# Early transposes kept in x, row factors in two steps, and a hand-ordered end: a change at both ends of a hybrid decoder trunk

## The chip, the cores and the metric

The kernel runs on one core of a Trainium2 chip. The core has five engines with instruction queues of their own: TensorE (PE, with its weight loads shown as PEld), VectorE (DVE), ScalarE (ACT), GpSimd (POOL) and SyncE (SP). SP issues nearly all loads here, ACT issues stores. TensorE writes to PSUM; the other engines read PSUM or the on-chip memory SBUF. The metric is the device time of one execution in microseconds (us); lower is better. A change of less than 0.5% (about 7 us) is not told apart from none here.

## The reference

One layer of a hybrid block on a sequence of 1024 rows of width 1024, then a final normalisation:

```python
mod = jax.nn.silu(c) @ ada_w + ada_b
shift, scale, gate = jnp.split(mod, 3, axis=-1)
h = rms_norm(x, norm_w) * (1 + scale[:, None, :]) + shift[:, None, :]
proj = h @ w_in
...  # two branches: y_a (gated spatial mixing) and y_b (state-space scan)
merged = jax.nn.sigmoid(g_a) * (y_a @ w_proj_a) + jax.nn.sigmoid(g_b) * (y_b @ w_proj_b)
return rms_norm(x + gate[:, None, :] * (merged @ w_out), final_norm_w)
```

The change touches the making of `h` and of the first products with `w_in` at the start, and the last product, `merged @ w_out`, with the final `rms_norm` at the end. The branches between are as before.

## The kernel before, in words

*Matrices and halves.* A row tile is 128 rows of x; there are eight (`xt[0]` to `xt[7]`), each with 1024 columns. The kernel needs h with its columns on the partitions, so every 128 x 128 piece is turned by a transpose on TensorE. A *block* is 128 columns of x; the eight blocks are worked in the order `KS = (0, 4, 1, 5, 2, 6, 3, 7)`, and "block n" below is place n of that order. A *half* `h` of a block is the row tiles 0 to 3 (`h = 0`) or 4 to 7 (`h = 1`). All products are made to fp32 precision from three products of a high and a low part, so that every row of h is also split in two (`hh`, `hl`).

*The first stage* (lines 168 to 457). `square(t)` sums the squares of a row tile on ACT, `factors` (L369) turns four sums at once into row factors with one small instruction on DVE (L371) and a power on POOL (L372), and `normed(t, half, eng)` (L374) scales 512 columns of a row tile in place (DVE L379 or ACT L377). `matvec(n)` multiplies 128 columns of the conditioning weights for shift and scale (`aw`, 1 MB a block in two buffers) on TensorE and copies the row; `modulation(n)` makes shift and scale of the block's columns from it. `transposes(n, h)` turns four pieces into a PSUM tile `px` (two buffers). `rows_of_h(n, h)` reads `px`, applies scale and shift in two ACT instructions (L297; for the very first block on DVE, L299 and L300), and subtracts to get the low part (DVE L301). `first_products(n)` is a generator of twelve products of a block, 128 x 512 each, six for a half; `split_w0(n)` prepares their weights (ACT L220, DVE L221).

The loop at L440 runs the twelve products of block n and, at set places between them, what block n + 1 needs (`prepare`, L403): for example `3: transposes(n, a)`, `5: modulation, rows_of_h(n, a)`, `9: transposes(n, b), rows_of_h(n, b)`, where a and b are the block's halves in the order in which it uses them. For block 1 a table of its own (L406) also holds the second half of block 0. The loads of block n + 2 are issued at the first product of block n. `warm(n)` issues products whose result nobody reads.

*What sets the order.* `pin` keeps an instruction in program order among the pinned ones of its engine. In the first stage nearly everything is pinned: its order on each engine is the order in the text. A planner lays out the instructions that are not pinned by a timing model; most of the vector, scalar and GpSimd work of the middle is of that kind. Waits between engines follow from the data, element by element; a tile's buffer goes to its next user when the last access has passed.

*The last stage* (L1651 to L1778). The last product is made as seven sub-products (`PRODUCTS`, L1711). Two of them matter here. `s4` completes columns 512 to 1023 of rows 0 to 511 (and the kernel finishes row tiles 4 to 7 beside it); `a12` completes columns 0 to 511 of row tiles 0 to 3 and is the last. `collect` (L1683) adds a PSUM tile to the row tile `r` on DVE and sums the squares on ACT; for row tiles 2 and 3 POOL multiplies the upper columns by the final weight `fnw` (L1691). `root(t)` makes one row factor with two 1-wide DVE instructions and a power on POOL (L1705 to L1707); `inv_root` (L1653) makes it on DVE by three Newton steps. `finish(t, y)` scales the row tile, whole on DVE (L1699) or, for tile 2, half on ACT (L1696) and half on DVE (L1697), and issues the store. Row tile 3 comes last, in two pieces of 256 columns (L1764 to L1778), with its factor by `inv_root`.

Of the kernel before, what the change touches and what calls it, by code (L numbers as in the profile page):

```python
# [16 lines left out]
P = 128  # L17
D = 1024
# [17 lines left out]
def hybrid_kernel(  # L36
# [131 lines left out]
    with tc.tile_pool(name="p0", bufs=1, reuse_waits="tile") as p0:  # L168
# [5 lines left out]
        xt = [p0.tile([P, D], F32, name=f"x{t}", tag=f"x{t}") for t in range(NCH)]  # L174
# [108 lines left out]

        def rows_of_h(n, h):
# [10 lines left out]
            if n + h:  # L295
                for t in (hh, hf):
                    pin(A.activation(t, px, AF.Identity, scale=md[:, 1:2], bias=md[:, 0:1]))  # L297
            else:
                pin(V.tensor_scalar(hf, px, md[:, 1:2], md[:, 0:1], op0=ALU.mult, op1=ALU.add))  # L299
                pin(V.tensor_copy(hh, hf))  # L300
# [68 lines left out]
        def factors(b):  # L369
            bs = slice(4 * b, 4 * b + 4)  # L370
# [69 lines left out]
        for n in range(KT):  # L440
            todo = prepare(n + 1) if n + 1 < KT else {}
            for at, _ in enumerate(first_products(n), 1):
                if at == 1 and n + 2 < KT:
# [1209 lines left out]
    def inv_root(n, w, other=None):  # L1653

        t, y, v = (dde[:, 8 * i + n : 8 * i + n + w] for i in range(3))
        if other is not None:
            V.tensor_scalar(t, part[:, n : n + 1], other, 1.0 / D, op0=ALU.add, op1=ALU.mult)
        else:
            V.tensor_add(t, part[:, n : n + w], part[:, 8 + n : 8 + n + w])
            V.tensor_scalar(t, t, 1.0 / D, EPS, op0=ALU.mult, op1=ALU.add)  # L1660
        V.tensor_scalar(y.bitcast(I32), t.bitcast(I32), -0.5, float(0x5F3759DF), op0=ALU.mult, op1=ALU.add)
        V.tensor_scalar_mul(v, t, -0.5)
        for _ in range(3):
            if w == 1:
# [148 lines left out]
```

## Time and profile before

| what | value |
|---|---|
| median of 3 runs | 1408.84 us (1404.32 to 1409.13) |
| the profiled execution | 1407.67 us, span 1405.9 us |
| TensorE busy | 1377.1 us, 98% of the span |
| DVE, ACT, POOL busy | 1062.4, 797.0, 213.0 us |
| granted TensorE clock, mean | 0.997 of full speed |
| data moved | 194.55 MB read, 87.46 MB written |

The span runs from the first to the last instruction of the trace; the profiled execution's own time is 1.8 us longer. A row of the trace in order of time gives the start in us, the duration, the engine, the line of the kernel, the operation, `output<-inputs`, the shape, and in brackets how long the engine had been idle and which work it had waited for. A line is often that of a helper (L81 is every product of the first stage, L84 every transpose, L90 every pinned load). `x4` means that four alike were merged. Instructions of one engine overlap a little at their ends, so that the distance between two starts is shorter than the duration. SPq and ACTq are the DMA issues of SP and ACT.

### The profile page before, as it was taken

How to read it: one execution, taken by the hardware profiler on the slowest of the kernel's cores; microseconds unless marked ns; L12 is line 12 of the kernel's file. 1: busy time of each engine (PE TensorE's matmuls, PEld its weight loads, DVE VectorE, ACT ScalarE, POOL GpSimd, SP SyncE). 2: the span in 40 equal slices, each digit the busy share in tenths (PEclk: the TensorE clock that was granted, in tenths of full speed). 3: DMA queues.
4: the chain of work that ended last, by engine and by line, in shares of the span. 5: the costliest groups of instructions: out<-in, count | busy, mean ns of one | idle time of the engine just before them, and what ended most of it. 6: DMA issues, size and time to landing. Idle time of an engine off the chain costs nothing.

```text
span 1405.9 us, 20633 instructions
## 1 busy us (share of the span) xinstructions
PE 1377.1 (98%) x7035; PEld 1139.9 (81%) x7035; DVE 1062.4 (76%) x1863; ACT 797.0 (57%) x1471; POOL 213.0 (15%) x208
## 2 busy tenths in 40 slices
PE   8999999999999999999999999999999999999997
PEld 6688888888888888888887888888888877878886
DVE  4786776777778889889788796388667767876976
ACT  5764576556656665556565555677766723322443
POOL 0000000000000011111000010038778740000001
PEclk9999999999999999999999999999999999999999
DMA  8653343343344777787675774598778749878903
GB/s 263 173 165 98 113 120 105 105 121 120 116 125 134 214 202 239 236 248 232 192 221 156 240 214 135 173 353 318 262 253 296 275 168 328 320 231 296 350 33 120
DMA packets 273150, 283.37 MB, mean 202 GB/s; under 512 B 15341, under 2 KB 223637, under 8 KB 273045
## 3 DMA queue, kind: packets, MB, share of 16 engines
q1 hardware_dynamic: 185684, 198.52, 44.4%
q10 hardware_dynamic: 87360, 83.54, 17.8%
q8 instruction: 55, 0.90, 0.3%
q14 instruction: 51, 0.41, 0.1%
HBM read 194.55 MB, written 87.46 MB: 201 GB/s over the span
## 4 chain that ended last, share of the span: by engine, by line
PE 80%; DMA 8%; DVE 5%; POOL 2%; issue 2%; ACT 1%; SPq 1%; ACTq 0%; DVEq 0%; POOLq 0%
PE xcb L574 6%; PE xuz L574 6%; PE xz L574 6%; PE xx L574 5%; PE xg L574 5%; PE x L1477 4%; PE yp L1477 4%; PE ox L1676 3%; PE yuz L574 3%; PE ycb L574 3%; PE pma L81 3%; PE xv L574 3%; PE yz L574 3%; PE yg L574 3%; PE yx L574 3%; DMA dcy<-acs_d 3%
## 5 line engine op out<-in xcount | busy, mean ns | idle before, releaser
L793 POOL TENSOR_TENSOR wog<-wog,gb 128x256 f32<-128x256 f32 x16 | 18.3, 1159 | 676.6 <-PE zz L574 413.3
L1007 ACT ACTIVATE dcy<-dcy,nacs 128x128 f32<-128x128 f32 x256 | 78.6, 388 | 14.9 <-POOL dcy L1002 14.5
L1002 POOL TENSOR_SCALAR_AFFINE_SELECT dcy<-dcy 128x1024 f32<-128x1024 f32 x32 | 35.0, 1095 | 135.7 <-ACT ea L999 132.3
L999 ACT ACTIVATE ea<-dcy 64x512 f32<-64x512 f32 x64 | 40.1, 626 | 14.2 <-DMA dcy<-acs_d 13.8
L920 ACT ACTIVATE ac<-ac 128x1024 f32<-128x1024 f32 x32 | 33.9, 1060 | 23.0 <-DVE ac L918 22.8
L81 PE MATMUL pma<-yh,wah 128*128 128x512 f32 x128 | 43.3, 419 | 0.0
L1027 DVE TENSOR_TENSOR dcy<-dcy,pc 128x1024 f32<-128x1024 f32 x32 | 39.0, 1218 | 4.8 <-PE pc L84 3.0
L81 PE MATMUL pma<-yh,wal 128*128 128x512 f32 x128 | 42.5, 413 | 0.0
L1089 POOL TENSOR_TENSOR yz<-y,sl 128x512 f32<-128x512 f32 x32 | 41.4, 1295 | 1.1
L1087 DVE TENSOR_TENSOR ym<-yn,ea 128x512 f32<-128x512 f32 (+1 forms) x32 | 19.9, 622 | 28.5 <-PE yn L81 28.3
L81 PE MATMUL pma<-yl,wah 128*128 128x512 f32 x128 | 40.1, 394 | 0.0
L1088 POOL TENSOR_TENSOR y<-y,ym 128x512 f32<-128x512 f32 (+1 forms) x32 | 36.6, 1144 | 14.4 <-DVE ym L1087 14.4
L81 PEld LDWEIGHTS yn<-sl,st 128*128 128x128 f32 x224 | 30.3, 190 | 8.3 <-issue 4.4
L81 PE MATMUL yn<-sl,st 128*128 128x128 f32 x224 | 31.6, 276 | 4.9 <-DVE st L1057 4.9
L1416 DVE SCALAR_TENSOR_TENSOR yn<-yn,par,rb 128x512 f32<-128x512 f32 x32 | 24.0, 749 | 15.7 <-DMA yn<-yb_d 15.5
L81 PE MATMUL sp<-xe,bn 128*128 128x256 f32 x112 | 32.6, 408 | 3.3 <-DVE ssq L1117 1.7
L81 PE MATMUL yi<-dcy,xd 128*64 128x128 f32 x512 | 35.7, 283 | 0.0
L918 DVE SCALAR_TENSOR_TENSOR ac<-c2x,cwt,ac 128x1023 f32<-128x1023 f32 (+2 forms) x24 | 31.2, 1300 | 5.3 <-ACT ac L916 5.1
L918 DVE SCALAR_TENSOR_TENSOR ac<-c2cb,cwt,ac 128x1023 f32<-128x1023 f32 (+2 forms) x24 | 31.1, 1296 | 4.4 <-ACT ac L916 4.3
L1691 POOL TENSOR_TENSOR r<-r,fnw 128x512 f32<-128x512 f32 x2 | 2.5, 1296 | 203.7 <-DMA out_dram<-r 203.7
L1055 POOL TENSOR_TENSOR st<-st,cd 128x256 f32<-128x256 f32 x48 | 32.1, 668 | 8.0 <-PE yn L81 5.3
L918 DVE SCALAR_TENSOR_TENSOR ac<-c1cb,cwt,ac 128x1023 f32<-128x1023 f32 (+2 forms) x24 | 31.6, 1318 | 1.3 <-ACT ac L916 1.3
(2980 smaller groups left out, 4390.9 us busy)
## 6 DMA issues: line engine op xcount, KB each, us to landing
sl<-s_d SPq DMA_DIRECT2D x32, 768.0 KB
s_d<-ac ACTq DMA_DIRECT2D x32, 512.0 KB
dcy<-acs_d SPq DMA_DIRECT2D x32, 512.0 KB
aw<-in_ada_w_dram SPq DMA_DIRECT2D x16, 512.0 KB
wbr<-in_w_proj_b_dram SPq DMA_DIRECT2D x64, 128.0 KB
wb_d<-wbb ACTq DMA_DIRECT2D x32, 256.0 KB
wb_d<-wbc ACTq DMA_DIRECT2D x32, 256.0 KB
yb_d<-yz ACTq DMA_DIRECT2D x32, 256.0 KB
```

What stands on the lines that cost most here:

```text
L81: pin(PE.matmul(acc, l, r, start=first, stop=last))
L574: pin(PE.matmul(ps, lw[:, k * P : (k + 1) * P], r[k], start=first and n + k == 0, stop=n == 2 and k == 3, skip_group_check=not first))
L918: V.scalar_tensor_tensor(ac[:, s:], cc[:, : S - s], conv_wt[:, 3 - s, i : i + 1], ac[:, s:], op0=ALU.mult, op1=ALU.add)
L920: A.activation(ac, ac, AF.Silu)
L999: A.activation(ea[hh * HD : (hh + 1) * HD], dcy.rearrange("p (j e) i l -> p e j (i l)", e=2)[hh * HD : (hh + 1) * HD, hh], AF.Exp)
L1002: G.affine_select(out=d8, in_=d8, compare_op=ALU.is_ge, fill=-1e30, base=0, pattern=[[0, 2 * HPG], [1, P]], channel_multiplier=-1)
L1007: A.activation(dcy[:, h, i, :], dcy[:, h, i, :], AF.Exp, bias=sub[:, i, h : h + 1])
L1027: V.tensor_tensor(d3, d3, pc[:, 0:256].unsqueeze(1).to_broadcast([P, HPG, 256]), op=ALU.mult)
L1088: G.tensor_add(y1[:, :, t0:], y1[:, :, t0:], m[:, :, t0:])
L1089: G.tensor_mul(yz, y1, sl[:, 4:6])
L1477: pin(PE.matmul(ps[j], a[:, v, js], r, start=first and n + k == 0, stop=n == 2 and k == KT - 1, skip_group_check=not first))
L1676: pin(PE.matmul(ps, a[:, tsl], b[:, cs], start=first and n + j == 0, stop=n == 2 and j == 3, skip_group_check=not first))
```

## The change

*Storage.* The eight tiles `xt` become two tiles of four row tiles each (`xq`); `xt[t]` is a view of them.

*Early transposes.* `turned(n, eng)` transposes half 0 of block n, and copies the PSUM tile back into x, over the columns it came from. It is called for blocks 2, 4, 1, 6, 3 and 5, ahead of the loop and between the first six products of block 0. The copies of 4 and 1 are on ACT, the others on DVE. In the loop, `transposes(n, 0)` is left out for blocks 1 to 6, and `rows_of_h(n, 0)` reads the copy in SBUF.

*Row factors.* `factors` takes a range: tiles 0 to 2 and then 3, tiles 4 to 6 and then 7. All scalings (`normed`) are now on DVE.

*Order of the first stage.* `matvec(0)` stands ahead of the scaling of the upper columns; the first six products of block 0 are drawn ahead of the loop; the second half of block 0 stands ahead of its seventh product; `matvec(1)` comes at the ninth product (it was the sixth), the rest of block 1 at the twelfth. There are 3, 5 and 4 warming products, where there were 3, 8, 6 and 5.

*The end.* POOL now multiplies the upper columns of row tiles 0 to 3 by `fnw`; `finish` splits tiles 0 to 3 between ACT and DVE; the last product `a12` is written out by hand and pinned, with each tile's finish one tile later than its sums; the last factor is a power on POOL in place of three Newton steps; for tile 3 only columns 0 to 255 are multiplied by `fnw` on POOL, 256 to 511 on DVE.

```diff
-        xt = [p0.tile([P, D], F32, name=f"x{t}", tag=f"x{t}") for t in range(NCH)]
+        xq = [p0.tile([P, 4, D], F32, name=f"xq{h}", tag=f"xq{h}") for h in range(2)]
+        xt = [xq[t // 4][:, t % 4] for t in range(NCH)]
...
+        four = lambda t: t.rearrange("p (i q) -> p i q", i=4)
+
+        def turned(n, eng):
+
+            transposes(n, 0)
+            part = xq[0][:, :, KS[n] * P : (KS[n] + 1) * P]
+            pin((A.copy if eng is A else V.tensor_copy)(part, four(pxs[n, 0])))
+            pxs[n, 0] = part
...
-                    pin(A.activation(t, px, AF.Identity, scale=md[:, 1:2], bias=md[:, 0:1]))
+                    pin(A.activation(four(t) if h == 0 and n in EARLY else t, px, AF.Identity, scale=md[:, 1:2],
+                                     bias=md[:, 0:1]))
...
-        def factors(b):
-            bs = slice(4 * b, 4 * b + 4)
+        def factors(a, b):
+            bs = slice(a, b)
...
-        for t in range(4):
-            square(t)
-        factors(0)
-        for t in range(4):
-            normed(t, 0, V)
+        for a, b in ((0, 3), (3, 4)):
+            for t in range(a, b):
+                square(t)
+            factors(a, b)
+            for t in range(a, b):
+                normed(t, 0, V)
         transposes(0, 0)
         split_w0(0)
+        matvec(0)
         for t in range(4):
             normed(t, 1, V)
-        matvec(0)
         warm(3)
         modulation(0)
-        warm(8)
+        turned(2, V)
+        warm(5)
         rows_of_h(0, 0)
+        start = first_products(0)
+        for i in range(6):
+            next(start)
+            if i == 1:
+                for t in range(4, 7):
+                    square(t)
+                factors(4, 7)
+                turned(4, A)
+            elif i == 3:
+                turned(1, A)
+            elif i == 5:
+                for n in (6, 3):
+                    turned(n, V)
+        for t in range(4, 7):
+            normed(t, 0, V)
+        turned(5, V)
+        square(7)
+        factors(7, 8)
+        for t in range(7, 8):
+            normed(t, 0, V)
         for t in range(4, NCH):
-            square(t)
-        factors(1)
-        for half in range(2):
-            for t in range(4, NCH):
-                normed(t, half, A if t > 5 else V)
-        split_w0(1)
+            normed(t, 1, V)
+        warm(4)
+        transposes(0, 1)
+        rows_of_h(0, 1)
+        EARLY = range(1, 7)
...
-                    6: lambda: (warm(6), transposes(0, 1), rows_of_h(0, 1), matvec(1), warm(5)),
-                    8: lambda: (transposes(1, 1), modulation(1), rows_of_h(1, 1)),
-                    12: lambda: (transposes(1, 0), rows_of_h(1, 0)),
+                    9: lambda: (matvec(1), split_w0(1), transposes(1, 1)),
+                    12: lambda: (modulation(1), rows_of_h(1, 1), rows_of_h(1, 0)),
...
+            early = lambda h: h == 0 and n in EARLY
...
-                3: lambda: transposes(n, a),
+                3: lambda: early(a) or transposes(n, a),
...
-                9: lambda: (transposes(n, b), rows_of_h(n, b)),
+                9: lambda: (early(b) or transposes(n, b), rows_of_h(n, b)),
...
-            if c and t in (2, 3):
+            if c and t < 4:
                 G.tensor_mul(r[:, cs], r[:, cs], fnw[:, cs])
...
-        if t == 2:
-            A.mul(r[:, 512:1024], r[:, 512:1024], y)
-            V.scalar_tensor_tensor(r[:, 0:512], r[:, 0:512], y, fnw[:, 0:512], op0=ALU.mult, op1=ALU.mult)
+        if t < 4:
+            pin(A.mul(r[:, 512:1024], r[:, 512:1024], y))
+            pin(V.scalar_tensor_tensor(r[:, 0:512], r[:, 0:512], y, fnw[:, 0:512], op0=ALU.mult, op1=ALU.mult))
...
+    def last_add(t, ps, cs, total):
+        r = rows[t]
+        pin(V.tensor_add(r[:, cs], r[:, cs], ps))
+        pin(A.activation(junk[:, cs], r[:, cs], AF.Square, accum_out=total))
+
+    lo, hi = slice(0, 256), slice(256, 512)
+    ps, r = acc["y"], rows[3]
+    for t in range(3):
+        for j in range(4):
+            out_products(ps[t], "a12", "b21", j, t, whole, True)
+        last_add(t, ps[t], whole, part[:, t : t + 1])
+        if t == 1:
+            finish(0, y0)
+        if t == 0:
+            y0 = root(0)
+        elif t == 1:
+            y1 = root(1)
+    for m, cs in enumerate((lo, hi)):
         for j in range(4):
             out_products(acc["xy"[m]][3][:, 0:256], "a12", "b21", j, 3, cs, True)
...
-    y = inv_root(3, 1, dde[:, 33:34])
-    V.tensor_scalar_mul(r[:, 0:512], r[:, 0:512], y)
+    finish(1, y1)
+    last_add(3, acc["x"][3][:, 0:256], lo, dde[:, 32:33])
+    y2 = root(2)
+    pin(G.tensor_mul(r[:, lo], r[:, lo], fnw[:, lo]))
+    pin(V.scalar_tensor_tensor(dde[:, 33:34], dde[:, 32:33], D * EPS, part[:, 11:12], op0=ALU.add, op1=ALU.add))
+    last_add(3, acc["y"][3][:, 0:256], hi, part[:, 3:4])
+    finish(2, y2)
+    v, y = dde[:, 34:35], dde[:, 35:36]
+    pin(V.tensor_scalar(v, part[:, 3:4], dde[:, 33:34], 1.0 / D, op0=ALU.add, op1=ALU.mult))
+    pin(G.tensor_tensor(y, v, nhalf[:, 0:1], op=ALU.pow))
+    pin(A.mul(r[:, 512:1024], r[:, 512:1024], y))
+    nc.scalar.dma_start(out[3 * P : 4 * P, 512:1024], r[:, 512:1024])
+    pin(V.scalar_tensor_tensor(r[:, hi], r[:, hi], y, fnw[:, hi], op0=ALU.mult, op1=ALU.mult))
+    pin(V.tensor_scalar_mul(r[:, lo], r[:, lo], y))
     nc.sync.dma_start(out[3 * P : 4 * P, 0:512], r[:, 0:512])
```

More of the change, by code (lines that the diff above doesn't have):

```diff
@@ L441, in hybrid_kernel @@
             todo = prepare(n + 1) if n + 1 < KT else {}
-            for at, _ in enumerate(first_products(n), 1):
-                if at == 1 and n + 2 < KT:
+            for at, _ in enumerate(first_products(n) if n else start, 1 if n else 7):
+                if at == (1 if n else 7) and n + 2 < KT:
                     load_aw(n + 2)
@@ L1651, in hybrid_kernel, with inv_root @@
     part = dthq[:, 0:16]
-    def inv_root(n, w, other=None):
+    def inv_root(n, w):
         t, y, v = (dde[:, 8 * i + n : 8 * i + n + w] for i in range(3))
[L1656 to L1660, printed above, removed]
+        V.tensor_add(t, part[:, n : n + w], part[:, 8 + n : 8 + n + w])
+        V.tensor_scalar(t, t, 1.0 / D, EPS, op0=ALU.mult, op1=ALU.add)
         V.tensor_scalar(y.bitcast(I32), t.bitcast(I32), -0.5, float(0x5F3759DF), op0=ALU.mult, op1=ALU.add)
@@ L1748, in hybrid_kernel @@
             continue
+        if nm == "a12":
+            break
         for t in range(4):
-            if nm == "a12" and t == 3:
-                break
             for j in range(4):
```

25 lines of the change are left out of this document (5 added, 20 removed).

## The prediction

> **What bounds the kernel now.** I read the page's head first, then the chain that ended last, then busy time by stretch, then the order of time at both ends of the kernel, which is where the diff is.
>
> ```profile
> span 1405.9 us, 20633 instructions
> PE 1377.1 (98%) x7035; PEld 1139.9 (81%) x7035; DVE 1062.4 (76%) x1863; ACT 797.0 (57%) x1471; POOL 213.0 (15%) x208
> PE 80%; DMA 8%; DVE 5%; POOL 2%; issue 2%; ACT 1%; SPq 1%; ACTq 0%; DVEq 0%; POOLq 0%
> 20.00:30.00 10.00, 9.05 (x67) 6.79 (x65) 3.90 (x11) 7.22 (x13) 1.02 (x1) 1.00 0.91 233
> 30.00:62.00 32.00, 31.82 (x243) 20.52 (x244) 23.76 (x52) 23.17 (x42) 0.00 (x0) 1.00 0.71 187
> ```
>
> The last two are rows of the view by stretches: length, then busy time of PE, PEld, DVE, ACT and POOL, the granted clock, DMA share and GB/s. TensorE carries the span (98%, 80% of the chain). From 30 to 62 us it is busy for 31.82 of 32 us, with DVE at 23.76 and ACT at 23.17: an instruction taken off PE there is time gained, as long as DVE and ACT follow. Before 30 us PE is filled up with warming products and waits for x, row factors and weights: there PE time is free, and the order on DVE, ACT and POOL counts. After PE's last product only a serial chain is left.
>
> **The change, head: how much it takes from PE.** Rows of PE in order of time, around one group of four transposes in block 1:
>
> ```profile
> 31.40 0.39 PE L81 MATMUL acc<-b22h,w0l 128*128 128x512 f32 x1
> 31.63 0.60 PE L84 MATMUL px<-ident,x 128*128 128x128 f32 x4
> 31.98 0.48 PE L81 MATMUL acc<-b22h,w0l 128*128 128x512 f32 x1
> ```
>
> Products come 0.23 apart (31.40 to 31.63); with the group between them, 0.58. A group thus costs 0.35 us. Six groups leave the block loop: that of block index 1 ran before 30 us, those of 2 to 6 ran in blocks 1 to 5, where PE is full. 5 x 0.35 = 1.75 us gained, if everything else keeps up. In exchange there are six copies (four on DVE, two on ACT) ahead of the loop, and rows_of_h then reads SBUF. Prices, from rows of the same shape a little later:
>
> ```profile
> 72.78 0.68 DVE L478 COPY dtt<-pd 128x512 f32<-128x512 f32 x1
> 75.41 0.58 ACT L590 COPY c1v<-xv 128x512 f32<-128x512 f32 x1
> 69.43 0.62 ACT L522 CAST p1v0h<-a11v 128x512 fp32r<-128x512 f32 x1
> ```
>
> A DVE copy out of PSUM is 0.68 (next one starts 0.60 later), an ACT one 0.58. An ACT read of SBUF is 0.62: 0.04 more, for twelve activations 0.5 us of ACT, hidden in its 9 idle us of the 32; if uncovered, one per block, 5 x 0.04 = 0.2 us. [...]
>
> **Head: what is late next.** The scalings, copies and factors are written out in order for each engine, so I follow DVE. Rows before:
>
> ```profile
> 10.04 0.19 ACT L367 ACTIVATION_READ_ACCUMULATOR junk<-x 128x1 f32 x1
> 11.89 1.03 POOL L372 TENSOR_TENSOR rs<-sq,nhalf 128x4 f32<-128x4 f32 x1 [10.16 <-DVE sq L371]
> 12.96 1.67 DVE L379 TENSOR_SCALAR x<-x,rs 128x512 f32<-128x512 f32 x4 [1.15 <-POOL rs L372]
> 16.71 0.41 DVE L263 COPY row<-pm 128x256 f32<-128x256 f32 x1
> 18.15 0.81 DVE L299 TENSOR_SCALAR hf<-px,md 128x512 f32<-128x512 f32 x1
> 18.99 0.43 DVE L300 CAST b11h<-hf 128x512 fp32r<-128x512 f32 x1
> 19.57 0.70 PE L81 MATMUL acc<-b11h,w0h 128*128 128x512 f32 x2
> 22.11 1.68 DVE L379 TENSOR_SCALAR x<-x,rs 128x512 f32<-128x512 f32 x4 [1.14 <-POOL rs L372]
> 24.87 0.77 ACT L297 ACTIVATE b<-px,md 128x512 fp32r<-128x512 f32 x1
> 28.84 0.49 PE L81 MATMUL acc<-b22h,w0h 128*128 128x512 f32 x1
> 30.07 1.07 PE L81 MATMUL pm<-aw,scz 128*32 128x256 f32 x16 [0.73 <-DMA aw<-in_ada_w_dram]
> 1390.60 0.55 POOL L1707 TENSOR_TENSOR dde<-dde,nhalf 128x1 f32<-128x1 f32 x1 [1.15 <-DVE dde L1706]
> ```
>
> *First tiles.* The third square ends at 10.23, the power on POOL takes 1.03 for four columns and 0.55 for one, so some 0.87 for three: three scalings of 0.42 run 11.43 to 12.68, the fourth, after its own factor (0.17 + 0.55 and hand-overs), ends at 13.90 instead of 14.63. That 0.7 us is spent again: DVE now holds its row copy until matvec(0) is through (15.3) with four scalings queued behind it (to 17.4), and the copy of block 2 (0.60) stands ahead of rows_of_h(0,0). Its cast then ends at 19.67 instead of 19.42: the first product runs at 19.8, 0.25 later.
>
> *Second tiles.* Before, DVE and ACT begin to scale x4..x7 at 22.11. After, PE has six products (0.23) with the groups of blocks 4, 1 and 6 (0.36) among them, from 19.8 to 22.3. DVE's queue holds, in this order, the copies of 6 and 3, three scalings, the copy of 5, the factor of tile 7 and only then the other scalings. So DVE, free at 20.6 and with the factors there at 21.6, waits for block 6's transposes until 22.45: copies to 23.65, scalings to 24.9, copy of 5 to 25.5, factor of tile 7 (0.17 + 0.55) to 26.4, its scaling to 26.8. transposes(0,1) end at 27.05 and ACT's first row of h starts there, not at 24.87: 2.2 us later. The 0.78 of that row gives the product at 27.9, matvec(1) behind three products at 28.6 (24 before); its row copy, w0's cast, modulation(1) and rows_of_h(1,1) bring block 1's first product to 32.4 against 28.84, and matvec(2) behind it to 32.6.
>
> What of it counts: before, matvec(2) stood at 30.07 for its weights anyway, so block 1 is late by 32.6 - 30.07 = 2.55, not 3.6. Against 1.75 gained, the head ends 0.8 us later. Bounds: no delay beyond the weights' arrival, -1.75; no gain left in the loop, +2.55. I take 0.8, which the rows add up to.
>
> *SP.* Loads for block index 3 wait for matvec(1) to release the buffer, so they are issued some 29.6 instead of 26. The load of index 2 took from 23.83, its issue, to 30.07, 6.2 us; 29.6 + 6.2 = 35.8, and matvec(3) wants it at 32.6 + 5.9 - 0.35 + 0.2 = 38.4. Queued behind it on SP are w0r of index 3, three small parameters and the loads of index 4: 2.6 us of cover; beyond that each microsecond costs one. Joining x into two tiles of four changes no address pattern that a load or product sees: nothing.
>
> **Tail.** Rows in order of time, before:
>
> ```profile
> 1395.84 1.28 DVE L1699 SCALAR_TENSOR_TENSOR r<-r,dde,fnw 128x1024 f32<-128x1024 f32 x1
> 1396.61 1.10 POOL L1771 TENSOR_TENSOR r<-r,fnw 128x256 f32<-128x256 f32 x1 [1.16 <-ACT junk L1770]
> 1396.62 0.28 PE L1676 MATMUL oy<-ms1h,mwhb 128*128 128x256 f32 x1
> 1397.04 0.68 DVE L1705 TENSOR_TENSOR dde<-dthq 128x1 f32<-128x1 f32 x1
> 1397.71 0.41 DVE L1769 TENSOR_TENSOR r<-r,oy 128x256 f32<-128x256 f32 x1
> 1398.21 0.42 ACT L1770 ACTIVATE junk<-r 128x256 f32<-128x256 f32 x1 [1.68 <-DVE dde L1706]
> 1398.89 1.19 DVE L1697 SCALAR_TENSOR_TENSOR r<-r,dde,fnw 128x512 f32<-128x512 f32 x1
> 1400.00 0.14 DVE L1661 TENSOR_SCALAR dde<-dde 128x1 int32<-128x1 int32 x1
> 1401.38 0.16 DVE L1669 SCALAR_TENSOR_TENSOR dde<-dde 128x1 f32<-128x1 f32 x1
> 1401.58 0.72 ACT L1777 ACTIVATE r<-r,dde 128x512 f32<-128x512 f32 x1 [2.02 <-DVE dde L1669]
> 1402.33 0.40 ACTq L1778 DMA_DIRECT2D out_dram<-r  x1
> ```
>
> PE's last product ends at 1396.90, but the last add starts at 1397.71, behind a 1024-wide finish and a 1-wide add that took 0.68 beside POOL's product. Then follow the square, a 1.19 us finish of row 2 and eight Newton steps (1400.00 to 1401.55). After: rows 0 to 2 are finished half on ACT (0.72) and half on DVE (some 0.64), so the last add can start at 1396.95 (+0.42), its square ends at 1397.9, row 2's half finish on DVE ends by 1398.0 (1398.5 if POOL slows it as in the 1.19 row), the sum 0.2, the power 0.55 with 0.1 of hand-overs: 1398.85 to 1399.35, ACT's product 0.72, and its store at 1399.6 to 1400.1 against 1402.33. That is -2.7 to -2.2; I take -2.5. Bounds: -2.8 with no contention; -1.5 where POOL's product of row 3 (up to 1.10) also holds the last add. The two further products on POOL and the ACT halves lie under PE's products of rows 0 to 2; uncovered they are 1.1 and 0.72 each.
>
> **Sum.** 1407.67 (the profiled execution: its span 1405.9 and 1.8 around it) + 0.8 - 2.5 = 1406.0. That execution lay 1.2 below the median 1408.84, so the median becomes 1407.1. The middle is untouched in the diff, yet what isn't pinned there is laid out by the planner anew: from the three runs shown (1404.32 to 1409.13) I allow 2 us either way.
>
> **The rivals.**
> *B, the head gains.* DVE's queue doesn't hold block 1 back; it starts where the weights of index 2 let it, as at 30.07. For it: the 0.73 wait on the DMA, and the freed ACT scalings. Against: the queue above. -1.75 - 2.5: 1404.6.
> *C, slower: the granted clock falls in the head.* At the end of the kernel it halves about 3 us after PE's last product:
>
> ```profile
> 1399.50:1400.00 0.50, 0.00 (x0) 0.00 (x0) 0.50 (x2) 0.06 (x1) 0.03 (x1) 0.89 0.00 0
> 1400.00:1402.00 2.00, 0.00 (x0) 0.00 (x0) 1.68 (x10) 0.42 (x1) 0.00 (x0) 0.50 0.54 217
> ```
>
> Between 23.7 and 27.9 PE would have only single transposes and four warming products, with 1.9 us empty at most; the clock before is 1.00 throughout 20 to 30. It decides once PE stands for 3 us. Products at half clock take 0.46: some 6 us of it until PE has been busy again cost 3 us: 1407.1 + 3 = 1410.1. [...]
> *D, the tail keeps its length.* POOL's product of row 3 and row 2's half finish meet, as in the 1.10 and 1.19 rows, and the planner's early finishes stay in DVE's way: tail -1.0, sum -0.2, 1408.6.
>
> **How the numbers follow.** Forecast 0.50, B 0.20, C 0.13, D 0.17. A change under 0.5% (7.0 us) is about what a measurement of this kernel can't tell from none. None of the four sums passes it; 0.05 on each side is for a planner's order of the middle that loses or wins more than I can price. Range: from B less the 2 us, 1402.5, to C with 1.5 more, 1411.5.
>
> **What would show it.** Right: block 1's first matvec of the loop (index 2) starting near 32.6 with no DMA wait, DVE idle before block 6's copy near 20.6 to 22.4, groups of four transposes gone from half of the places between 30 and 62 us, the first pair's products (70.3 before) about 0.8 later, and the last ACT store under 3.3 us behind PE's last product, against 5.4. Wrong: matvec(2) again near 30, a granted clock under 1 between 20 and 40 us, a wait on the weights of index 3, or a middle whose length moves by more than the two ends.

## The result, and the profile after

| | median of 22 runs | range | profiled span | TensorE instructions |
|---|---|---|---|---|
| before | 1407.38 us | 1401.95 to 1415.04 | 1405.9 us | 7035 |
| after | 1411.38 us | 1406.3 to 1415.86 | 1409.7 us | 7015 |

The changed kernel is slower by the ratio 1.0034, 95% interval 1.0024 to 1.0045: some 4 to 5 us, where 1.7 us less was forecast. Both ends of the kernel did about what the prediction said of them. The loss lies between them, where the program is the same. With 22 runs on each side the interval is 0.1% wide to either side, so this difference, though under the 0.5% named at the start, is told from none. *TensorE instructions* are its product entries as the page counts them; each has a weight load beside it (PEld x7015 in the changed kernel), and one warming product makes two entries (`warm(36)` is x72 in the trace of before).

From the page of the changed kernel: span, busy time of the engines, share of the chain that ended last by engine.

```profile
span 1409.7 us, 20602 instructions
...
PE 1375.1 (98%) x7015; PEld 1136.1 (81%) x7015; DVE 1065.6 (76%) x1866; ACT 794.1 (56%) x1471; POOL 218.8 (16%) x212
...
PE 33%; DMA 7%; DVE 5%; ACT 4%; issue 3%; POOL 3%; SPq 1%; ACTq 0%; POOLq 0%; DVEq 0%
```

TensorE is busy for 2.0 us less than before and the span is 3.8 us longer: PE waits more. Next the head by stretches (columns as in the prediction), and rows of it in order of time.

```profile
20.00:30.00 10.00, 7.30 (x58) 5.17 (x57) 5.99 (x15) 3.70 (x7) 1.40 (x2) 1.00 0.82 208
30.00:62.00 32.00, 30.56 (x223) 19.06 (x225) 23.89 (x53) 24.55 (x45) 0.00 (x0) 1.00 0.71 196
```

```profile
22.41 1.29 DVE L291 COPY xq<-px 128x512 f32<-128x512 f32 x2 [2.32 <-PE px L84]
...
26.19 2.07 DVE L390 TENSOR_SCALAR xq<-xq,rs 128x512 f32<-128x512 f32 x5 [0.65 <-POOL rs L383]
...
28.83 1.07 PE L81 MATMUL pm<-aw,scz 128*32 128x256 f32 x16
...
32.77 0.51 PE L81 MATMUL acc<-b22h,w0h 128*128 128x512 f32 x1 [1.25 <-ACT b22h L307]
33.20 1.07 PE L81 MATMUL pm<-aw,scz 128*32 128x256 f32 x16
...
39.27 1.07 PE L81 MATMUL pm<-aw,scz 128*32 128x256 f32 x16
```

DVE stands for 2.32 us before block 6's copy, block 1 starts at 32.77, and its matvec at 33.20 without a wait on a DMA, 3.13 us behind the 30.07 of before. The loop gives 1.95 of that back: at 79 us PE is 1.18 us late. The tail, in order of time:

```profile
1402.74 0.28 PE L1702 MATMUL oy<-ms1h,mwhb 128*128 128x256 f32 x1
...
1403.06 0.42 DVE L1791 TENSOR_TENSOR r<-r,oy 128x256 f32<-128x256 f32 x1 [0.15 <-PE oy L1702]
...
1404.36 0.54 POOL L1818 TENSOR_TENSOR dde<-dde,nhalf 128x1 f32<-128x1 f32 x1 [0.75 <-DVE dde L1817]
...
1404.94 0.72 ACT L1819 ACTIVATE r<-r,dde 128x512 f32<-128x512 f32 x1 [0.30 <-POOL dde L1818]
...
1405.69 0.41 ACTq L1820 DMA_DIRECT2D out_dram<-r  x1
```

The last add starts 0.32 us behind the start of the last product (1.09 before), the last ACT store 2.95 behind it (5.71 before). From that product's start to the end of the span it is 6.96 us (1409.7 - 1402.74); before it was 9.28 (1405.9 - 1396.62). The tail is 2.3 us shorter.

So the ends sum to 1.2 - 2.3 = -1.1 us, and the span grew by 3.8. The missing 4.9 us lies between 79 us and the last product in these two executions. Up to the last stage the program there has its instructions in the same order on all five engines in both kernels. I matched TensorE's instructions of the two traces one by one; this is how late each kernel's are, start minus start in the kernel before, in us (one profiled execution each; the lower rows belong to the experiments):

```
                     count halves  at 79   345   500   601   661   960  1081  1382 us
after                 7015   1     1.18  1.18  2.90  2.96  5.11  5.57  3.95  5.49
after_again           7015   2     1.83  1.83  1.83  1.83  2.71  1.32 -0.05  2.69
after_fill4           7015   1     2.32  2.31  3.63  4.10  5.78  5.94  3.53  3.94
after_moved5          7015   1     1.97  1.99  2.04  2.04  2.81  1.87 -0.70  3.97
after_pad8early       7031   2     3.88  3.87  3.92  4.93  5.84  4.92  2.65  4.07
after_pad_early       7035   2     4.79  4.79  4.79  4.79  4.79  3.45  0.14  4.79
after_pad10           7035   0     1.32  1.32  1.33  1.32  1.33  0.76 -3.42 -5.38
head_only             7015   2     3.33  3.32  4.65  4.86  7.03  5.93  5.37  7.62
tail_only             7035   0    -0.09 -0.09 -0.09  1.27  1.27  1.16 -1.93 -2.15
before_less10         7015   0     0.37  0.37  1.15  1.39  3.30  3.17  0.99  2.95
mended_head           7035   1    -0.33 -0.30 -0.30 -0.30 -0.30 -1.40 -6.40 -5.99
mended_again          7035   1     1.51  1.57  1.61  2.59  2.59  1.20 -1.34 -1.96
mended_less10         7015   1    -0.35 -0.35 -0.34  0.69  3.09  3.41  0.95  3.75
mended_less10_again   7015   0     0.42  0.42  1.47  2.09  4.13  5.30  3.63  3.45
mended_more5          7045   0     0.32  0.31  0.31  1.04  2.71  3.40  3.11  3.44
mended_less15         7005   2     0.63  0.63  0.63  1.94  2.11  2.12  2.05  2.98
```

*count* is the number of TensorE instructions, *halves* how often the granted clock stood at a half for 3.41 us between 79 and 1382 us; the kernel before has one, at 1031 us. Ahead of 79 us it did so too in head_only (at 28.7 us), after_fill4 (20.4), after_pad8early (29.6), after_pad_early (28.0, for 6.83 us), mended_again (33.3), mended_less10_again (32.1) and mended_less15 (32.4), which explains most of the large figures in the first column.

What a half costs in the middle can be read here: from 1000 to 1040 us the nine executions without one in that stretch gain 3.9 us on the kernel before in the median, the seven with one 1.9, so a half costs some 2 us. The changed kernel has one, as the kernel before has, and its 4.3 us are not the clock. But two executions of one program differ: in after_again, which is the changed kernel again, the middle is only 0.9 us longer, with two halves. One profile places a loss; how large it is in general, the medians say.

In its first profile the changed kernel loses 5.49 - 1.18 = 4.3 us from 79 to 1382 us, and 0.6 more in the last stage. It comes in steps, and at the two large ones PE waits for an engine that a late transfer had put behind. Both of them, in order of time:

```profile
347.27 0.34 SPq L90 DMA_DIRECT2D vm<-v_d  x1
...
362.96 2.66 DVE L796 SCALAR_TENSOR_TENSOR gacc<-ag,sc,gacc 128x1024 f32<-128x1024 f32 x2 [1.46 <-DMA ag<-in_ada_w_dram]
364.28 0.58 ACT L622 COPY c1x<-xx 128x512 f32<-128x512 f32 x1 [3.71 <-DVE gacc L796]
364.92 1.21 PE L606 MATMUL xx<-t2h,p6x2h 128*128 128x512 f32 x4 [1.39 <-ACT c1x L622]
...
618.97 0.37 SPq L90 DMA_DIRECT2D a11g<-in_w_in_dram  x1
...
631.01 0.30 ACT L857 CAST wba<-wbr 128x128 fp32r<-128x128 f32 x1 [4.44 <-DMA wbr<-in_w_proj_b_dram]
631.34 0.29 DVE L862 TENSOR_TENSOR wba<-wbr,wba 128x128 fp32r<-128x128 f32 x1 [2.42 <-ACT wba L857]
...
637.42 0.67 DVE L622 TENSOR_TENSOR c2z<-p5z,xz 128x512 f32<-128x512 f32 x1
638.15 1.19 PE L606 MATMUL xz<-t4h,p4z2h 128*128 128x512 f32 x4 [1.55 <-DVE c2z L622]
```

The same places before, and the stretch of the second by the view of stretches:

```profile
344.14 0.34 SPq L90 DMA_DIRECT2D vm<-v_d  x1
...
612.30 0.37 SPq L90 DMA_DIRECT2D a11g<-in_w_in_dram  x1
...
624.40 0.30 ACT L825 CAST wba<-wbr 128x128 fp32r<-128x128 f32 x1 [2.16 <-DMA wbr<-in_w_proj_b_dram]
```

```profile
500.00:661.00 161.00, 161.00 (x712) 133.37 (x711) 140.87 (x257) 93.54 (x161) 18.54 (x15) 1.00 0.80 241
```

SP's load of a11g is issued 6.67 us later, while PE at 601 us is only 2.96 late: the transfers have fallen behind the work. ACT's cast of wba then waits 4.44 us in place of 2.16, DVE stands for 2.42 us behind that cast, and c2z, further back in DVE's queue, is what PE waits for: it stands for 1.55 us in these 161 us, where it was busy for all of them before.

### The profile page after: what moved, and what is told of

Read it like the earlier page. It is cut to its first block, busy times and chain, and to the rows that moved or that the text cites. A ratio compares the mean times of both kernels' runs of the same rounds, so it can differ in the third digit from the quotient of the medians.

```text
span 1409.7 us, 20602 instructions
## 1 busy us (share of the span) xinstructions
PE 1375.1 (98%) x7015; PEld 1136.1 (81%) x7015; DVE 1065.6 (76%) x1866; ACT 794.1 (56%) x1471; POOL 218.8 (16%) x212
## 4 chain that ended last, share of the span: by engine, by line
PE 33%; DMA 7%; DVE 5%; ACT 4%; issue 3%; POOL 3%; SPq 1%; ACTq 0%; POOLq 0%; DVEq 0%
PE x L1509 5%; PE yp L1509 4%; PE ox L1702 3%; PE xz L606 3%; PE xg L606 3%; DMA dcy<-acs_d 2%; PE pma L81 2%; PE xcb L606 2%; PE yg L606 2%; PE oy L1702 1%; PE yz L606 1%; PE xx L606 1%; DMA yn<-yb_d 1%; ACT dcy L1039 1%; DMA wbr<-in_w_proj_b_dram 1%
## 5 line engine op out<-in xcount | busy, mean ns | idle before, releaser
L81 PE MATMUL sp<-xe,bn 128*128 128x256 f32 x112 | 32.6, 408 | 3.1 <-DVE ssq L1149 1.9
L1087 POOL TENSOR_TENSOR st<-st,cd 128x256 f32<-128x256 f32 x48 | 32.4, 676 | 8.0 <-PE yn L81 5.1
```

What stands on the lines that cost most here:

```text
L81: pin(PE.matmul(acc, l, r, start=first, stop=last))
```

## The experiments

The theory at first: the ends are as predicted, and the middle lost time by how the two kernels' streams lie against the transfers. What the two streams differ in ahead of the middle is their length: ten warming products fewer make 20 TensorE instructions fewer (7015 against 7035, the weight loads not counted). Rivals: the clock halves in the emptied stretch of the head; the move of the transposes itself loses more than the head shows; the whole is a matter of single executions or chips.

**One end alone.** *tail_only* is the kernel before with the new end; against the changed kernel it has the old storage and first stage:

```diff
-        turned(2, V)
-        warm(5)
+        warm(8)
         rows_of_h(0, 0)
-        start = first_products(0)
...
-                3: lambda: early(a) or transposes(n, a),
+                3: lambda: transposes(n, a),
```

*head_only* is the changed kernel with the old end:

```diff
-    pin(G.tensor_tensor(y, v, nhalf[:, 0:1], op=ALU.pow))
...
+    y = inv_root(3, 1, dde[:, 33:34])
```

> The first stage of before, the end of the change. All theories: the distance from TensorE's last product to the end of the span falls by 2.3 us (9.3 to 7.0), as in the changed kernel's trace. The theory that places of TensorE's instruction fetches make the middle longer (fetch): the stream ahead of the middle is that of before, so the middle, from the product of p3v0h into yv (79.4 us) to the product of t4 (1370.3 us), keeps its 1290.9 us within 1 us, and the time falls by 2 to 2.5 us (some 1405 against a before of 1407.4). The rival that the new end itself costs in the middle or ahead of the last product: the time does not fall.

> The first stage of the change, the end of before. All theories: the middle begins 1.2 us late, as in the changed kernel's trace. Fetch, and the rival that the late first blocks put the loads of the middle behind (head): the middle is 4 to 5 us longer again, so that the time rises by 5 to 7 us (some 1413 to 1414). The rival that the longer middle was chance in one execution (chance): the middle within 1.5 us of 1290.9, time up by 1.2 us (1408.6).

Measured: tail_only 0.9986 (0.9968 to 1.0003), span 1402.1; head_only 1.0035 (1.0020 to 1.0051), span 1413.6. In tail_only's trace the end's gain is there by itself (6.95 us from the start of the last product to the end of the span); its runs alone don't tell it from nothing. The loss comes with the head. In the profiled execution of head_only the clock did halve. The view by stretches, head_only:

```profile
24.00:28.00 4.00, 2.19 (x16) 1.56 (x14) 3.35 (x10) 0.29 (x1) 0.54 (x1) 1.00 0.86 246
28.00:33.00 5.00, 4.46 (x26) 2.37 (x27) 1.87 (x5) 1.83 (x4) 0.00 (x0) 0.66 0.20 53
```

A mean of 0.66 over 5 us is 3.4 us at a half. Its first stage ends 3.33 us late, not 1.18: the halving cost 2.15.

**The number of warming products.** Their results are read by nobody, so every kernel here computes the same. *after_pad10* gives the changed kernel ten more, *before_less10* takes ten from the kernel before.

```diff
-        warm(5)
+        warm(10)
...
-        warm(4)
+        warm(9)
```

```diff
-        warm(8)
+        warm(3)
...
-                    6: lambda: (warm(6), transposes(0, 1), rows_of_h(0, 1), matvec(1), warm(5)),
+                    6: lambda: (warm(3), transposes(0, 1), rows_of_h(0, 1), matvec(1), warm(3)),
```

> The changed kernel with ten warming products more, five each at two places where TensorE stood idle (5 to 10 and 4 to 9), so that its stream is as long ahead of the middle as before's. Fetch: the 16 KB packets of instructions fall in the middle where they fell before (the one at 345.2 us of the changed kernel back to 339 to 340), the middle returns to 1291 within 1.5 us, and the time falls by 4 us against the changed kernel, to some 1407, 0 to 1 below before. Head and chance: no change against the changed kernel, 1411.4, 4 above before.

> The kernel before with ten warming products fewer (8 to 3, 6 to 3, 5 to 3), all else as it was: its first stage keeps its time (matvec of block index 2 waits for its weights at 30.07 us in any case). Fetch: the packets move by 5 to 7 us against the work, as in the changed kernel, the middle becomes 3 to 5 us longer, time 1411 to 1412 (4 above before). Head and chance: the time of before, 1407.4 within 1.5.

Measured: after_pad10 0.9971 (0.9955 to 0.9988), span 1398.8; before_less10 1.0008 (0.9991 to 1.0025), span 1408.9. Ten products that do nothing, 0.14 us of them visible in the head (1.32 late at 79 us, 1.18 without them), make the changed kernel faster than the one before. From 79 us on nothing differs in the program up to the last stage, and it is 1.32 + 5.38 = 6.7 us shorter from there to 1382 us than the kernel before, of which some 2 us are the clock (no half against one). The other direction fails its expectation: 3 to 5 us were expected of before_less10, its time is not told from that of before, and its interval ends at 1.0025, 3.5 us. Its one profile has the middle 2.6 us longer; by the runs, the count alone makes less on the kernel before than what the changed kernel lost.

**Again, and the clock.** *after_again* is the changed kernel unchanged. *after_pad_early* adds ten narrow products (20 instructions, 32 columns wide; ten such instructions took 1.28 us in mended_head, as did ten of the usual form in the changed kernel) behind `warm(5)`; *after_moved5* moves five warming products from the start into the sparse stretch before 28 us, with their number as it is (`warm(36)` becomes `warm(31)`, `warm(4)` becomes `warm(9)`); *after_fill4* moves four from just ahead of the first product into it. The edits of after_pad_early and of after_fill4:

```diff
         warm(5)
+        for _ in range(10):
+            mm(accs[1][1][0:32, 0:P], scz[:, 0, :], ones)
```

```diff
-        warm(5)
+        warm(1)
...
-        warm(4)
+        warm(8)
```

> The changed kernel once more, for a second profile and for times on the same chip as the three others. 3 to 4.5 us above before. Fetch: the same steps in the middle (near 372 and 633 us), the section from 79 to 960 us 3 to 4.4 us longer than before's. The theory that the granted clock falls in the sparse stretch of the new first stage (clock), as it did in head_only's profile (half speed for 3.4 us from 28.7): half speed for 3.4 us between 25 and 35 us in some executions, 2 us each; this profile may or may not show it.

> The changed kernel with twenty records more in TensorE's stream, made of ten products with 32 columns of weights, all right behind the warming products that follow block index 2's early transposes, where TensorE is idle; nothing is added in the sparse stretch from 23 to 28 us. Fetch: the middle is as short as after_pad10's (79 to 960 us within 1.5 us of before's), time 4 to 6 us under after_again. Clock: no change against after_again, since the sparse stretch is as it was.

> The changed kernel with five warming products moved from the first batch (36 to 31) to the one in the sparse stretch (4 to 9): TensorE's stream ahead of the middle has the changed kernel's length, the sparse stretch is filled as in after_pad10. Clock: no half speed before 40 us, time as after_pad10's against before, 4 us under it or 7 under after_again. Fetch: the section from 79 to 960 us stays 2.5 to 4.4 us longer than before's; time at most 2 us under after_again (what the clock cost in the mean).

> The changed kernel with four warming products moved from the batch behind block index 2's early transposes (5 to 1) to the sparse stretch (4 to 8): the stream keeps its length, and the order of every other engine's instructions is the changed kernel's to the last row (that was not so in after_moved5 and after_pad_early, where some forty vector instructions of the late middle changed places). Clock: no half speed before 40 us, and 2 us or more under the changed kernel (some 0.15% above before or less). Fetch: no better than the changed kernel, 0.25 to 0.4% above before, apart from at most 1 us for the clock.

Measured: after_again 1.0018 (1.0002 to 1.0035); after_pad_early 1.0010 (0.9994 to 1.0027); after_moved5 1.0036 (1.0019 to 1.0052); after_fill4 1.0040 (1.0027 to 1.0053). Filling the sparse stretch with the count left alone gained nothing. By itself after_fill4 doesn't settle the clock: taking four products from ahead of the first one opened another gap there (an estimated 2.4 us, from the wait of 1.37 there in the changed kernel and 1.06 for eight of its warming instructions), and its profile has the half at 20.4 us, against the expectation. The granted clock on record of every run does. Within the runs of one kernel a mean clock lower by 0.001 goes with 1.1 us (fitted over the 324 runs); the 22 runs of the changed kernel have 0.9965 in the mean, those of after_moved5 0.9965, those of the kernel before 0.9964 to 0.9970 on the three chips of the experiments. By that slope the clock makes at most an estimated half a microsecond of the 4, so the clock is not what makes the changed kernel slow. It has a share in other differences: after_pad10's runs had 0.9979, worth an estimated 1.5 of its 7.7 us below the changed kernel. In after_pad_early and after_moved5 the planner also put 41 DVE and 6 ACT instructions of the late middle in another order, so they say less; the first also had its clock halved at 28.0 us and a head 4.79 us late. In after_again the step at 364 us is gone and its middle grew by 0.9 us only: neither a single step nor the 4.3 us of one execution is fixed to a program.

**The count without a reordering.** *after_pad8early* has eight such narrow products (16 instructions), which leave the order elsewhere untouched and the sparse stretch as sparse.

```diff
+        for _ in range(8):
+            mm(accs[1][1][0:32, 0:P], scz[:, 0, :], ones)
```

> The changed kernel with sixteen records more (eight products with 32 columns of weights) where TensorE is idle ahead of the first product, the sparse stretch as it was, the order of the other engines as the changed kernel's to the last row. Fetch: 3 to 5 us under the changed kernel, that is at or up to 2 us under before, with the section from 79 to 1081 us shorter than before's by 2 us or more, as in after_pad10 and after_pad_early. Clock: as the changed kernel, 0.25 to 0.4% above before.

Measured: 0.9990 (0.9978 to 1.0003), 6.6 us (1406.46 against 1413.10) under after_fill4 on the same chip; the two intervals don't touch. The granted clock (0.9966 against 0.9955) makes an estimated 1.2 us of it. Its profiled execution does not show the gain in the span (1408.2: a halved clock at 29.6 us put its head 3.88 us late, and its middle grew by 0.2 us in place of 4.3); the section from 79 to 1081 us is 1.2 us shorter than before's, where 2 or more was expected.

**A head without the queue.** *mended_head* takes away what the prediction found late in the head: one factor for tiles 4 to 7, their scalings ahead of the copies, the copies of blocks 6 and 3 on ACT, and enough warming products to bring the count to 7035 (nineteen, five of them narrow, where the changed kernel has nine; not the fifteen that the text below names).

```diff
-                for t in range(4, 7):
+                for t in range(4, NCH):
                     square(t)
-                factors(4, 7)
+                factors(4, 8)
...
                 for n in (6, 3):
-                    turned(n, V)
+                    turned(n, A)
...
+        for t in range(4, NCH):
+            normed(t, 1, V)
+        turned(5, V)
```

> The changed kernel with the first stage in another order: one factor for tiles 4 to 7, the scalings ahead of the copies of blocks 6, 3 and 5 in DVE's queue (6 and 3 on ACT), and fifteen warming products in place of nine there, so that TensorE's stream is as long as before's. If the prediction's reading of the queue on DVE is right, block index 1 starts near 29.4, matvec of index 2 waits for its weights near 30.1 to 30.4 us, and the middle begins 1.4 us earlier than before (2.5 earlier than after_pad10): time 6 us under before, near 1401. If something else holds the first blocks back, it begins as late as the changed kernel's, and the time is after_pad10's, 4.5 under before.

Measured: 0.9961 (0.9947 to 0.9974), 1400.36 us, the fastest kernel of the study. Rows of it in order of time:

```profile
22.77 3.25 DVE L390 TENSOR_SCALAR xq<-xq,rs 128x512 f32<-128x512 f32 x8 [1.14 <-POOL rs L383]
...
31.25 0.50 PE L81 MATMUL acc<-b22h,w0h 128*128 128x512 f32 x1 [1.25 <-ACT b22h L307]
31.68 1.07 PE L81 MATMUL pm<-aw,scz 128*32 128x256 f32 x16
```

Block 1 starts 1.5 us earlier than in the changed kernel, but at 31.25, not near 29.4, and matvec of index 2 still has no wait for its weights: the queue on DVE was part of the delay only, and what else holds block 1 is not isolated. PE is 0.33 early at 79 us, not 1.4 as expected. The larger part of its gain came again from the middle (5.7 us from 79 to 1382 us, with one half as in before).

**The count again, on the mended head.** From here the order on every engine is the same in all versions; only warming products differ. *mended_less10* has ten fewer (7015 instructions), *mended_more5* five more (7045), *mended_less15* fifteen fewer (7005); *mended_again* and *mended_less10_again* are repeats. The last four ran on one chip and share their runs of the kernel before.

The edit of mended_less10:

```diff
-        warm(10)
+        warm(5)
...
-        for _ in range(5):
-            mm(accs[1][1][0:32, 0:P], scz[:, 0, :], ones)
```

mended_less15 has `warm(0)` and no narrow products either; mended_more5 has `warm(15)` and keeps them.

> mended_head with ten warming products fewer (10 to 5, and the five narrow ones left out), so that the stream ahead of the middle has the changed kernel's length again; the order of all other engines as mended_head's. Fetch: 3 to 4 us above mended_head, some 0.15% under before, with the section from 79 to 1081 us 3 us longer than mended_head's. Clock and head: mended_head's time within 1 us, 0.39% under before, unless the profile shows half speed in the first 40 us.

> The mended head once more, unchanged, beside three versions of it on one chip that differ from it only in how many warming products stand in TensorE's stream before 27 us (their results are read by nobody; the order of the work on every engine is the same). Theory that the length of the stream ahead of the middle decides: again 0.995 to 0.998 of the kernel before. Rival, that the first figure (0.9961) was a matter of the chip or the hour: all four versions agree within 0.0015 of one another, whatever that common value is.

> Ten warming products (20 records) fewer than the mended head, unchanged from its first run. Stream theory: 3 to 8 us slower than the mended head on this chip, 0.998 to 1.002 of the kernel before. Rival: within 2 us of the mended head.

> Five warming products (10 records) more than the mended head, ahead of the first product; they take about 0.6 us there, of which 0.26 us is a wait already. Stream theory: the first stage up to 0.4 us later and the middle's length off the mended head's by more than 1 us; it gives no sign, since it doesn't say which meetings come and go. Rival: 0 to 0.5 us slower than the mended head, from the first stage alone.

> Fifteen warming products (30 records) fewer than the mended head: none stay ahead of the first product. Stream theory: like the version with ten fewer or worse, 3 to 9 us slower than the mended head. Rival: within 2 us of the mended head, plus up to 2 us if a granted clock of a half appears in the emptied stretch before 27 us.

| kernel | TensorE instructions | ratio to before (95% interval) |
|---|---|---|
| mended_head; mended_again | 7035 | 0.9961 (0.9947 to 0.9974); 0.9964 (0.9948 to 0.9980) |
| mended_more5 | 7045 | 1.0006 (0.9989 to 1.0023) |
| mended_less10; mended_less10_again | 7015 | 1.0005 (0.9988 to 1.0022); 1.0004 (0.9990 to 1.0019) |
| mended_less15 | 7005 | 1.0007 (0.9991 to 1.0023) |

The two repeats fall on their first figures, that of the mended head on another chip. Fewer products and more both cost 0.4%, 5 to 6 us, and none of the three other counts is told from the others. So it is not the fewer the worse: 7035, which is also the count of the kernel before, is better than each neighbour tried. The clock is not the reason: the runs of mended_less10_again and mended_more5 had 0.9981 in the mean, those of mended_again 0.9975, and were slower all the same; with 0.9962 it makes an estimated 1.4 of mended_less15's 5 us. One place of the middle separates the counts without exception: from 601 to 661 us the five profiles with 7035 lose 0.00 to 0.01 us on the kernel before, the eleven with another count 0.17 to 2.4. The loss can be followed. Page and rows of mended_head:

```profile
PE 1375.5 (98%) x7035; PEld 1138.3 (81%) x7035; DVE 1064.3 (76%) x1863; ACT 797.1 (57%) x1473; POOL 218.7 (16%) x211
```

```profile
612.13 0.37 SPq L90 DMA_DIRECT2D a11g<-in_w_in_dram  x1
...
624.22 0.30 ACT L855 CAST wba<-wbr 128x128 fp32r<-128x128 f32 x1 [2.28 <-DMA wbr<-in_w_proj_b_dram]
```

```profile
500.00:661.00 161.00, 161.00 (x712) 133.30 (x711) 140.47 (x258) 93.15 (x161) 20.10 (x16) 1.00 0.81 242
```

And of mended_less10:

```profile
PE 1376.1 (98%) x7015; PEld 1136.0 (81%) x7015; DVE 1063.6 (76%) x1863; ACT 795.5 (57%) x1473; POOL 217.3 (15%) x211
```

```profile
617.42 0.37 SPq L90 DMA_DIRECT2D a11g<-in_w_in_dram  x1
...
629.14 0.30 ACT L853 CAST wba<-wbr 128x128 fp32r<-128x128 f32 x1 [4.13 <-DMA wbr<-in_w_proj_b_dram]
```

```profile
500.00:661.00 161.00, 158.77 (x697) 130.15 (x696) 136.37 (x253) 88.39 (x155) 17.61 (x15) 1.00 0.77 231
```

PE stands at the same place in both until 500 us (-0.30 and -0.34 in the table of shifts). By 612 us the load of a11g is 5.29 us later in mended_less10, with a DMA share of 0.77 against 0.81 over the stretch, ACT's cast waits 4.13 in place of 2.28, and PE stands for 2.23 us of these 161. This is the place, and nearly the numbers, of the changed kernel's loss (6.67 us late, a wait of 4.44). Shown is that the length of a middle that is the same depends on how many warming products stand ahead of it, in the changed and in the mended kernel. By which path is not shown, nor that the number itself, rather than something that goes with it, decides: the candidate is told in the last section, and wasn't isolated.

## Why the prediction was wrong

*The head: right.* +0.8 was predicted, +1.2 measured. Its places: matvec(1) 28.6 against 28.83, block 1's first product 32.4 against 32.77, matvec(2) 32.6 against 33.20 without a wait on its weights, DVE's wait for block 6 to 22.45 against 22.41, the loop's gain 1.75 against 1.95. SP's later loads had the cover that was worked out: matvec(3) at 39.27 waits for nothing. The rows of h read from SBUF cost about what was priced (0.04 us more each): for the same output 0.80 us against 0.77 from PSUM (f32), 0.81 against 0.78 (fp32r). That the queue on DVE is the whole reason for the late block 1 is not borne out: without it, in mended_head, block 1 came 1.5 us earlier, not 3.4.

*The tail: right.* -2.5 predicted, -2.3 measured, the last ACT store 2.67 us behind the end of the last product (1402.74 + 0.28), where 5.4 was before and under 3.3 was asked for.

*The failed step* is in the sum: "The middle is untouched in the diff, yet what isn't pinned there is laid out by the planner anew: from the three runs shown (1404.32 to 1409.13) I allow 2 us either way." The planner did not lay it out anew; and the middle term, put at 0 with 2 us about it, measured +4.9 in the profiled execution (+4.3 from 79 to 1382 us, +0.6 from there to the last product), and by the medians about as much (4.0 + 1.1). It outweighed both ends, and turned the sign; the last of the prediction's own signs of being wrong, a middle whose length moves by more than the two ends, is what came. The step took the scatter of runs of one program for the difference between two programs whose streams have another length. With it failed "there PE time is free", said of the filled stretch before 30 us: ten warming products put back there (after_pad10) brought the same kernel from 1.0034 to 0.9971. That the number of these products is the cause is shown for the changed kernel; the path from there to the later transfers stays open, and so does why before_less10 lost so little.

*The rivals.* B, the head gains: fell; matvec(2) came at 33.20, not 30. D, the tail keeps its length: fell, 2.3 us shorter. C, the halved clock in the sparse stretch: it happens, in the profiled execution of head_only among others, but not in the changed kernel's own (1.00 in both stretches above). It cost 2.15 us there, where 3 was priced. That price came from some 6 us at a half until PE has been busy again, an estimate of the author's. No run shows that length: the clock stood at a half for 3.4 us in head_only and for 6.83 in after_pad_early, and what ends it is not shown. In head_only the 16 products of matvec(1) took 1.94 us at a half, against 1.07 at 28.83 in the changed kernel. Nor did PE have to stand for 3 us: in head_only its longest wait between 25 us and the half at 28.7 was 1.47 us, and in the middle the clock halved at 1031.25 us behind a wait of 2.77 us (before), at 1033.85 behind one of 2.33 (the changed kernel). The mean clock of the changed kernel's runs is that of before's (0.9965 against 0.9964 to 0.9970). So it sets single executions, not the difference.

*The result against the chances.* The median lies within 0.5% of the kernel before, on the side that was not forecast. It lies within the range by 0.1 us (1411.38 against 1411.5), and that is luck: this end of the range was made for C, which is not what happened.

## What to carry to other kernels

A stretch that a change leaves alone, instruction by instruction, is not a stretch whose time is unchanged: where transfers fill it (0.8 of the DMA engines here from 500 to 661 us), ten warming products more or fewer ahead of it moved two of the three kernels tried by 0.4% and 0.6%, and the third by less than could be told from nothing. Filler is part of a tuned schedule: after taking some out, put the count back as a test before judging the real edit; here the same edit, with its queue on DVE mended and its count restored, went from 1.0034 to 0.996. And match the two traces instruction by instruction before looking for a reason: the lateness by place told the ends from the middle at once. Take more than one profile of each, and look where the clock was halved in it, before a figure of the middle is believed.

## What was not expected of the hardware

TensorE's instructions come as transfers through the same DMA engines. From the section on DMA queues in the changed kernel's page, and from the DMA view of it between 341.7 and 348 us:

```profile
q8 instruction: 55, 0.90, 0.3%
```

```profile
q10 hardware_dynamic: 528, 0.52, 24.8%
q8 instruction: 1, 0.02, 1.0%
```

55 packets of 16 KB for 7015 products, each with its weight load, are one for about 128 products, and one takes about 1 us (1.0% of 16 engines over 6.3 us). That they are TensorE's is read from their times, which keep pace with its products: from 128 to 403 us there are 10 for 1275 products, from 948 to 1138 us 11 for 1384, one for 128 and one for 126, though the first stretch is 275 us long and the second 190. In the changed kernel one falls on the end of a 512 KB store at 345 us, behind which SP issues the next loads at 347.27; before, none fell between 340.5 and 345 us, and SP issued them at 344.14. With 20 instructions fewer the fetches come at another place of the work: in mended_less10 2 to 6 us later than in mended_head between 119 and 399 us, while PE stands at the same place. That is a path by which the count could act. Two things speak against a single meeting: in mended_less10 and in after_again a fetch also falls near there (343.7 and 346.0 us) and PE loses nothing; and in mended_more5 the fetches around 600 us come where mended_head has them (593.9 and 623.4 us against 594.4 and 623.1), and PE loses 1.7 us from 601 to 661. So no single meeting is shown to carry the loss. Why 7035 in particular is good stays open, and so does what makes the middle of the mended head and of after_pad10 3.5 to 6.7 us shorter than that of the kernel before, with the same 7035; of the 6.7, which is after_pad10's, some 2 are the clock.
